# A mixer's queries, keys and decays in three tiles instead of one, another order of its score levels, and waits by tile for reused pool space

## The chip, the cores and the metric

The kernel runs on one core of a Trainium2 chip, in one launch. The metric is the device time of an execution in microseconds (us). Before the change it is 1374.46 us, the median of three runs (1373.4 to 1375.46). One more execution was profiled; its own time is 1371.81 us, of which the profile's span covers 1370.0 us.

In the profile PE is TensorE's matmul side and PEld its weight loads, DVE is VectorE, ACT is ScalarE, POOL is GpSimd, and SP is the engine whose queue issues most DMAs. L729 is line 729 of the kernel.

## The reference, cut to what matters

One layer of a streaming encoder runs on a prompt of 1024 tokens and, with its own stored states, on 32 further tokens (the decode rows). All in float32:

```python
h, st_new = mixer(rms_norm(x, g_mix_pre[l]), st, ...)      # in-projection, three kinds of heads, out-projection
x = x + rms_norm(h, g_mix_post[l])
h, ffn_buf = conv_ffn(rms_norm(x, g_ffn_pre[l]), ...)      # up, causal conv of 3, gelu(gate) * value, down
x = x + rms_norm(h, g_ffn_post[l])
```

Six GLA heads and five HGRN2 heads share one recurrence with a decay per key channel, computed in blocks of 64 tokens:

```python
b = jnp.cumsum(ac, axis=1)
diff = b[:, :, None] - b[:, None, :]
decay = jnp.where(mask, jnp.exp(jnp.where(mask, diff, 0.0)), 0.0)
scores = jnp.einsum('bihd,bjhd,bijhd->bijh', qc, kc, decay)
o = (jnp.einsum('bijh,bjhv->bihv', scores, vc)
     + jnp.einsum('bihk,bhkv->bihv', qc * jnp.exp(b), s))
s_new = (jnp.exp(b_last)[..., None] * s
         + jnp.einsum('bjhk,bjhv->bhkv', kc * jnp.exp(b_last[:, None] - b), vc))
```

Five mLSTM heads have a scalar decay per token, a normaliser and a running maximum. Each kind's output is normalised per head and gated; the three together (`cat`) go through `w_out`.

## The kernel before, in words

Every large product is made of three fp32r products, high by high, low by high and high by low (lines 101 to 103), so PE carries about 11,500 matmuls.

**Stages.** The tokens are cut into units of 128: u = 0 to 7 of the prompt, and u = 8, the 32 decode rows. Units 0 to 2, 3 to 5, and 6, 7 and 8 are three groups. `inproj` (from line 357) normalises and projects a group and writes its queries, keys and decays to DRAM (`qkb_d`, or `qkbs_d` for unit 8). `mixer(u)` (from line 719) is a generator; its pieces are merged into the program beside the in-projection of the next group, and those of the last group (in the order u8, u6, u7) beside the out-projection (`outproj`, from line 1055). Then come the FFN's up-projection and down-projection. Matmuls of a mixer are queued with `soon` and taken one by one between those of the large products. The order on each engine is fixed when the program is built, by a scheduler that works with a model of the durations; every engine then takes its own instructions strictly in that order, and waits in front of the first that isn't ready.

**A mixer.** Lines 727 to 731 load one tile `qkb` (1536 columns, one buffer) by two DMAs, first the decays `b`, then queries `q` and keys `k` together; slices of it are called q4, k4 and b4. ACT takes eb = exp(b) (L771), DVE forms kh (L787, L790) and qz = q*eb (L781), and ACT makes `qe`, four scaled copies of parts of q (L812, one buffer). The scores are built by levels: level c pairs the second half of each block of 2c tokens with its first half. `operands(c)` (lines 814 to 840) subtracts decays on DVE (L825), takes two exponentials on ACT (L827, L828), and writes Ld (L830) and Qz (L835, L839); level 1 needs one exponential (L833, L834), and PE reads its keys straight from k4. The levels are taken in pairs, since there are two buffers of Qz and Ld. PE multiplies (L717) and DVE puts a level's result into P by `copy_predicated` (L805). After the last pair come z = q*k for the diagonal (L930), og and oh (the outputs, from P and from the states), om and oi (the mLSTM heads), and `finish` (squares L988, sums L989, POOL's reciprocal root L220 and L221, gated `cat` L991 and L993). Two heads' results are kept in the same PSUM banks, so om waits until og has been read by DVE (L991).

**Names that the prediction uses.** pv and pf are PSUM banks of the in-projection, pb transposes values vf (ACT copies them at L468) that had been projected in the other orientation; vth, vg and g_d are the gates on their way to DRAM (L427, L429, L431, L432), which a mixer loads again as gt (L743). wt_* are in-projection weights, wor the out-projection's (L689, eight loads of 512 KB), split into woh (ACT, L107 and L1049) and wol (DVE, L110 and L1051). ctp, ch and cl are the transposed `cat` (L1075, L1079, L1080), zp the out-projection's banks, z0, z1 their contents, fxt the transposes of the result. jk is the discarded output of the Square that gives a unit's norm (L303); gh is a broadcast row of gains.

Of the kernel before, what the change touches and what calls it, by code (L numbers as in the profile page):

```python
# [8 lines left out]
F32 = mybir.dt.float32  # L9
F32R = mybir.dt.float32r  # L10
BF16 = mybir.dt.bfloat16
# [3 lines left out]
PSUM = bass.MemoryType.PSUM  # L15
# [18 lines left out]
SUBS = [(0, 272), (272, 256)]  # L34
# [5 lines left out]
def fcol(u):  # L40
# [51 lines left out]
def body(ctx: ExitStack, tc: tile.TileContext, a: dict):  # L92
    nc = tc.nc
    act, dve, pool, pe, sp = nc.scalar, nc.vector, nc.gpsimd, nc.tensor, nc.sync
# [19 lines left out]


    dr = ctx.enter_context(tc.tile_pool(name="dr", bufs=1, space=DRAM))
    cp = ctx.enter_context(tc.tile_pool(name="cp", bufs=1))
    psb = ctx.enter_context(tc.tile_pool(name="psb", bufs=3, space=PSUM))
    mxs = ExitStack()
    mx = mxs.enter_context(tc.tile_pool(name="mx", bufs=1, side="left"))  # L120
    psm = mxs.enter_context(tc.tile_pool(name="psm", bufs=2, space=PSUM))
    pfs = ExitStack()
    pf = pfs.enter_context(tc.tile_pool(name="pf", bufs=1, side="left"))
    p1s = ExitStack()
    p1 = p1s.enter_context(tc.tile_pool(name="p1", bufs=1, side="right"))
# [131 lines left out]
    pws, wo_raw, ring = ExitStack(), [], []  # L257
# [99 lines left out]
    def inproj(g, xh, xl, normed, scaled=None):  # L357
# [4 lines left out]
        def t1(tag, bufs=1, w=T, dt=F32):  # L362
            return pf.tile([128, w], dt, tag=tag, name=f"{tag}_{g}", bufs=bufs)
# [290 lines left out]
        q = t1("q", 2)  # L654
# [4 lines left out]
        for t, f in ((4, 1), (5, 2)):  # L659
            ps = feat(t)  # L660
            q = t1("q", 2)
# [5 lines left out]
        q = t1("q", 2)  # L667
# [12 lines left out]

        if g == 2:
            pfs.close()
            pw = pws.enter_context(tc.tile_pool(name="pw", bufs=1, side="left"))
            ring.append(lambda name: pw.tile([128, 1024], F32, tag="ring", name=name, bufs=NRING))
            for k in range(8):
                if k == CT0:
                    load_cat(0)
                wo_raw.append(ring[0](f"wor{k}"))
                sp.dma_start(wo_raw[k], a["w_out"][k])  # L689
# [29 lines left out]
    def mixer(u, g, ci0):  # L719
        n = 128 if u < 8 else DEC  # L720
# [3 lines left out]
        nch = len(chunks)  # L724
        levels = [c for c in LEVELS if 2 * c <= cl]

        qkb = mx.tile([128, 1536], F32, tag="qkb", name=f"qkb{u}", bufs=1)
        for s0, s1 in ((2, 3), (0, 2)):
            sp.dma_start(qkb[:, 4 * n * s0:4 * n * s1],  # L729
                         (qkb_d[u] if u < 8 else qkbs_d)[:, s0:s1].rearrange("p a f n -> p (a f n)"))  # L730
# [11 lines left out]
        gt = mx.tile([128, 1024], F32, tag="gt", name=f"gt{u}", bufs=1)  # L742
# [65 lines left out]
        qe = mx.tile([128, 2, 2, 128], F32, tag="qe", name=f"qe{u}", bufs=1)  # L808
# [46 lines left out]
        cat = mx.tile([128, 1024], F32, tag="cat", name=f"cat{u}", bufs=1) if u != 7 else ring[0]("cat7")  # L855
# [563 lines left out]
    praw, ph, EARLY = [], [], 3  # L1419
# [79 lines left out]
    def down_all(ph, pc, begun, late):  # L1499
# [6 lines left out]
        ssp = late.enter_context(tc.tile_pool(name="p11", bufs=1, side="right"))  # L1506

        def w_banks(name):
            return [psf.tile([128, 512], F32, tag="sx", name=f"{name}0", bufs=1)] + \
# [74 lines left out]
        s1 = psf.tile([128, 512], F32, tag="xw", name="s1", bufs=4)  # L1584
# [55 lines left out]

        run("P7", X, False, True, lambda p, w: residual(p))
        late.close()
        px_ = late.enter_context(tc.tile_pool(name="p12", bufs=1, side="right"))
        xres = {}
        for u in range(4):
            xres[u] = px_.tile([128, 1024], F32, name=f"fr{u}")
# [31 lines left out]
    side = []  # L1678
# [34 lines left out]
        side.append(mixers(g))  # L1713
    p1s.close()
    p2s = ExitStack()
    p2 = p2s.enter_context(tc.tile_pool(name="p2", bufs=1, side="right"))
    wo = outproj_setup(p2)
    wo += (out_weights(wo),)
    p3s = ExitStack()

    x0 = p3s.enter_context(tc.tile_pool(name="p3", bufs=1, side="right")).tile([128, 8, 2, SUBS[0][1]], F32, name="xg0")
    xlate[0] = x0
    n0, n1 = SUBS[0][1], SUBS[1][1]
    smp = DEC // 2
# [11 lines left out]


    p4s, p5s, p6s, p7s, p8s, p9s, pxs, phs, late = (ExitStack() for _ in range(9))
    p0 = p4s.enter_context(tc.tile_pool(name="p4r", bufs=1, side="left"))
    p4 = p4s.enter_context(tc.tile_pool(name="p4", bufs=1, side="left"))  # L1740
    px = [pxs.enter_context(tc.tile_pool(name=f"px0{i}", bufs=1, side="left")) for i in range(2)]
    psf = p4s.enter_context(tc.tile_pool(name="psf", bufs=1, space=PSUM))
    praw += [p0, p4]
    upper.append(psf)
    raw0 = up_raw(0)
    pt = p5s.enter_context(tc.tile_pool(name="p5", bufs=1, side="left"))
    tail.append(lambda name: pt.tile([128, 1024], F32, tag="tail", name=name, bufs=3))
    own = {"c1": pt.tile([128, SUBS[0][1]], F32, name="c1_00")}
    jks.append(own["c1"].bitcast(BF16)[:, :512])
# [14 lines left out]
        with tc.issue_after(kept["c1"].ins):  # L1764
            next(last[1])
    p3s.close()
    tp = p6s.enter_context(tc.tile_pool(name="p6", bufs=1, side="left"))
# [5 lines left out]
    p7 = p7s.enter_context(tc.tile_pool(name="p7", bufs=1, side="right"))  # L1773
# [7 lines left out]
    for u in uus[0]:  # L1781
        pool.memset(u[:, 0:2], 0.0)
    p7.tile([128, 8], F32, name="pad1")
    px1 = p8s.enter_context(tc.tile_pool(name="px1", bufs=1, side="right"))
    py = []
    X.append(None)
    begun = {}

    def freed():
        pxs.close()  # L1790
        ph.append(phs.enter_context(tc.tile_pool(name="ph", bufs=1, side="left")))
# [10 lines left out]
    for i, _ in enumerate(up_all(pw_, W0, X, uus, lambda: py[0], freed, ahead, blk)):  # L1802
        if i == 1:

            with tc.issue_after(done[0].ins), tc.issue_after(kept["c6"].ins):
                for x in last:
                    next(x)
            X[1] = col_operands([px1] * 2, {f"B{k + 1}{j + 1}": x1[:, 4 * k:4 * k + 4, j, :] for k in range(2) for j in range(2)}, 1)
            p6s.close()
            p5s.close()  # L1810
            py.append(p9s.enter_context(tc.tile_pool(name="p9", bufs=1, side="right")))
    sp.dma_start(a["p_fc"], fhalo)
    sp.dma_start(a["q_fc"], fcache)
    p9s.close()
    p8s.close()
    p7s.close()
    p10 = p8s.enter_context(tc.tile_pool(name="p10", bufs=1, side="right"))
    down_all(ph[0], p10, begun, late)
    late.close()
    p8s.close()  # L1820
# [131 lines left out]
```

## Time and profile before

| what | before |
|---|---|
| time, median of 3 runs | 1374.46 us (1373.4 to 1375.46) |
| time of the profiled execution | 1371.81 us |
| its span | 1370.0 us |
| PE busy | 1309.2 us, 96% of the span |
| PEld, DVE, ACT, POOL busy | 1191.7, 1030.3, 704.6 and 329.9 us |
| in-projection with the mixers of units 0 to 5 | to about 513 us |
| out-projection with the mixers of units 8, 6 and 7 | about 513 to 655 us |
| FFN | from about 682 us to the end |

A row of the timeline gives start and length in us, engine, line, operation and tiles, and in square brackets how long the engine had been idle before it and what it waited for. PEclk is the clock granted to TensorE as a share of full speed.

### The profile page before, as it was taken

Reading aid. Unit: us, or ns where it says so; the run is one execution under the profiler, and the core shown is the slowest. Engines: PE = TensorE matmul, PEld = TensorE weight load, DVE = VectorE, ACT = ScalarE, POOL = GpSimd, SP = SyncE. Lnnn points to the kernel's source line nnn. Section 1 sums busy time; section 2 is a strip of 40 time slices with the busy share of each in tenths; the row PEclk is TensorE's granted clock in tenths of the full one; section 3 lists DMA queues with packets and bytes.
Section 4 is the critical chain, followed back from the end, with each engine's and each line's share of the span. In section 5 each row is a group of like instructions: output and inputs, shape, how many; then the busy total and the mean of one; then the engine's idle time right before and its main releaser. Section 6 shows DMA issues by size and latency. Waiting matters only on the chain.

```text
span 1370.0 us, 29214 instructions
## 1 busy us (share of the span) xinstructions
PE 1309.2 (96%) x11472; PEld 1191.7 (87%) x11472; DVE 1030.3 (75%) x1916; ACT 704.6 (51%) x1368; POOL 329.9 (24%) x529
## 2 busy tenths in 40 slices
PE   6999999998998989998989999999999999999997
PEld 5999989998897977777889999999999997678885
DVE  4786559678597757796788888888888876399566
ACT  4555556555474535353665455545555544454552
POOL 5532403135022154133231112121121110010005
PEclk9999999999999999999999999999999999999999
DMA  9599878786789935535413465555365239644425
GB/s 344 204 322 352 288 270 252 266 281 219 261 247 315 328 102 202 158 115 155 149 43 132 145 176 149 150 137 161 111 171 136 85 131 390 262 156 134 149 105 123
DMA packets 125825, 269.72 MB, mean 197 GB/s; under 512 B 24007, under 2 KB 59367, under 8 KB 125607
## 3 DMA queue, kind: packets, MB, share of 16 engines
q1 hardware_dynamic: 111959, 245.43, 52.4%
q0 software_dynamic: 8928, 18.09, 7.2%
q10 hardware_dynamic: 4800, 4.33, 0.9%
q8 instruction: 90, 1.47, 0.4%
q14 instruction: 48, 0.39, 0.1%
HBM read 206.72 MB, written 86.18 MB: 214 GB/s over the span
## 4 chain that ended last, share of the span: by engine, by line
PE 65%; DVE 13%; DMA 8%; ACT 7%; issue 3%; POOL 3%; SPq 1%; ACTq 0%; DVEq 0%; POOLq 0%
PE pux L103 5%; PE pux L102 5%; PE pux L101 5%; PE puw L102 3%; PE puw L103 3%; PE puw L101 3%; PE q L101 3%; PE q L102 3%; PE q L103 3%; PE pv L101 3%; PE pv L103 2%; PE x L101 2%; DMA qkb<-qkb_d 2%; PE pv L102 2%; PE x L102 2%
## 5 line engine op out<-in xcount | busy, mean ns | idle before, releaser
L1375 DVE SCALAR_TENSOR_TENSOR y<-uu,fconv_sb,y 128x1060 f32<-128x1060 f32 x88 | 116.3, 1321 | 37.0 <-ACT y L1373 36.5
L1311 ACT COPY c<-pux 128x272 f32<-128x272 f32 (+1 forms) x132 | 49.3, 375 | 49.7 <-PE pux L103 49.0
L101 PE MATMUL pv<-wt_0h,xh 128*128 128x256 f32 (+2 forms) x195 | 57.5, 295 | 6.0 <-ACT xh L321 2.6
L101 PE MATMUL zp<-woh,ch 128*128 128x512 f32 (+1 forms) x144 | 59.1, 411 | 2.6 <-issue 1.4
L1373 ACT ACTIVATE y<-uu,fconv_sb 128x1060 f32<-128x1060 f32 x44 | 56.0, 1273 | 7.8 <-POOL uu L1369 7.5
L103 PE MATMUL zp<-woh,cl 128*128 128x512 f32 (+1 forms) x144 | 57.7, 401 | 1.3 <-DVE cl L1080 1.3
L1372 POOL COPY fhalo<-uu 128x2 f32<-128x2 f32 x44 | 16.5, 375 | 174.5 <-DVE uu L1316 174.4
L102 PE MATMUL zp<-wol,ch 128*128 128x512 f32 (+1 forms) x144 | 58.0, 402 | 0.0
L103 PE MATMUL pv<-wt_0h,xl 128*128 128x256 f32 (+2 forms) x195 | 56.0, 287 | 0.2 <-DVE xl L322 0.2
L103 PE MATMUL pv<-wt_1h,xl 128*128 128x256 f32 (+2 forms) x195 | 56.1, 288 | 0.0
L102 PE MATMUL pv<-wt_0l,xh 128*128 128x256 f32 (+2 forms) x195 | 55.9, 287 | 0.1
L101 PE MATMUL pv<-wt_1h,xh 128*128 128x256 f32 (+2 forms) x195 | 55.7, 286 | 0.0
L102 PE MATMUL pv<-wt_1l,xh 128*128 128x256 f32 (+2 forms) x195 | 55.6, 285 | 0.0
L1551 POOL TENSOR_TENSOR gss<-gss 128x1 f32<-128x1 f32 (+1 forms) x9 | 8.3, 923 | 186.4 <-ACT gjk L1544 186.4
L220 POOL TENSOR_SCALAR hrs<-hss 128x5 f32<-128x5 f32 (+3 forms) x27 | 10.7, 396 | 175.9 <-DVE hss L989 175.2
L805 DVE COPY_PREDICATED P<-masks_sb,sc 128x352 f32<-128x352 int32 (+3 forms) x53 | 37.8, 714 | 11.8 <-PE sc L717 10.7
L101 PEld LDWEIGHTS pv<-wt_0h,xh 128*128 128x128 f32 (+1 forms) x195 | 36.8, 189 | 8.1 <-ACT xh L321 3.3
L431 POOL TENSOR_TENSOR vg<-vth,gh 128x256 f32<-128x256 f32 (+1 forms) x36 | 28.6, 796 | 59.4 <-DVE vth L427 34.3
L1369 POOL COPY uu<-uu 128x2 f32<-128x2 f32 x44 | 31.4, 714 | 43.6 <-DVE uu L1316 42.7
L221 POOL TENSOR_TENSOR hrs<-hrs,mhalf 128x5 f32<-128x5 f32 (+3 forms) x27 | 39.3, 1454 | 2.3
L993 POOL TENSOR_TENSOR cat<-cat,gt 128x320 f32<-128x320 f32 (+3 forms) x27 | 31.3, 1161 | 29.5 <-DVE cat L991 29.4
L102 PEld LDWEIGHTS pv<-wt_0l,xh 128*128 128x128 f32 (+1 forms) x195 | 36.9, 189 | 0.6 <-POOL wt_0l L110 0.5
(1714 smaller groups left out, 5330.7 us busy)
## 6 DMA issues: line engine op xcount, KB each, us to landing
wrP<-in_w_dn SPq DMA_DIRECT2D x27, 512.0 KB, 3.3
h_d<-y SPq DMA_DIRECT2D x22, 530.0 KB, 2.8
ht<-h_d SPq DMA_DIRECT2D x22, 530.0 KB, 7.8
wt_0r<-in_w_tok SPq DMA_DIRECT2D x21, 512.0 KB, 11.2
wt_1r<-in_w_tok SPq DMA_DIRECT2D x21, 512.0 KB, 5.1
ws_d<-in_w_dn POOLq DMA_DIRECT2D x20, 512.0 KB, 9.6
wrP<-ws_d SPq DMA_DIRECT2D x20, 512.0 KB, 4.5
wt_0l<-lt_d SPq DMA_DIRECT2D x14, 512.0 KB, 7.6
```

The lines of the kernel that those rows point to most:

```text
L101: pe.matmul(ps, lh[0], rh[0], start=first, stop=False, **kw)
L102: pe.matmul(ps, lh[0], rh[1], start=False, stop=False, **kw)
L103: return pe.matmul(ps, lh[1], rh[0], start=False, stop=last, **kw)
L221: pool.tensor_tensor(out, out, mhalf[:n, :cols], op=ALU.pow)
L431: pool.tensor_tensor(o[:n], th[:n], gh[:n, c0:c0 + 256], op=ALU.mult)
L805: dve.copy_predicated(dst, mk.broadcast_to([n, 11, *mk.shape[2:]]), src)
L993: pool.tensor_tensor(cat[:n, c0:c0 + 64 * nh], cat[:n, c0:c0 + 64 * nh], gt[:n, c0:c0 + 64 * nh], op=ALU.mult)
L1311: kept[name] = act.copy(t, ps)
L1369: pool.tensor_copy(u[:, GAP_P:GAP_P + 2], u[:, GAP_S - 2:GAP_S])
L1372: behind["POOL"] = pool.tensor_copy(fhalo[:, j, :], u[:, NCOL - 2:NCOL])
L1373: act.activation(y, u, AF.Identity, scale=fconv[:, j, 2:3], bias=fconv[:, j, 3:4])
L1375: dve.scalar_tensor_tensor(y, uu[i][:, s:s + NCOL], fconv[:, j, s:s + 1], y, op0=ALU.mult, op1=ALU.add)
```

## The change

It has four parts.

- **Tiles.** q, k and b become three tiles of 512 columns with a DMA each, in the order q, b, k. q has two buffers, k and b have one. The sizes of the pool allow it because gh moves from the pool `mx` to `p1`, and the Squares' jk of units 3 to 8 moves from a buffer of its own in `p1` into the one buffer of `qe` (unit 2's uses k's).
- **Levels.** 32, 16 | 8, 4 | 2, 1 becomes 32, 16 | 2, 1 | 8, 4. For unit 8, whose blocks are 32 long, 16, 8 | 4, 2 | 1 becomes 16, 2 | 1, 8 | 4.
- **Waits.** Every pool gets `reuse_waits="tile"`: a tile on space of a closed pool waits for the tiles that lay there.
- **Order.** The scheduler gives another order with these: 771 of 9677 PE rows move, 470 of 1918 on DVE, 190 of 1352 on ACT, 21 of 534 on POOL, and SP has nine more DMAs and 60 rows moved. All lies before the FFN's up-projection, whose order and that of everything behind it is as before. The instructions of compute are otherwise the same in kind and number. Lines from 731 on have one number less.

```diff
-LEVELS = [32, 16, 8, 4, 2, 1]
+LEVELS = [32, 16, 2, 1, 8, 4]
...
-    mx = mxs.enter_context(tc.tile_pool(name="mx", bufs=1, side="left"))
+    mx = mxs.enter_context(tc.tile_pool(name="mx", bufs=1, side="left", reuse_waits="tile"))
...
-    gh = mx.tile([128, 1024], F32, name="gh")
+    gh = p1.tile([128, 1024], F32, name="gh")
...
-                jk = mx.tile([128, 1024], BF16, tag=("gt", "cat", "qkb")[u], name=f"jk{u}", bufs=1)
+                jk = mx.tile([128, 1024], BF16, tag=("gt", "cat", "k")[u], name=f"jk{u}", bufs=1)
             else:
-                jk = p1.tile([128, 1024], BF16, tag="jk", name=f"jk{u}", bufs=1)
+                jk = mx.tile([128, 1024], BF16, tag="qe", name=f"jk{u}", bufs=1)
...
-        qkb = mx.tile([128, 1536], F32, tag="qkb", name=f"qkb{u}", bufs=1)
-        for s0, s1 in ((2, 3), (0, 2)):
-            sp.dma_start(qkb[:, 4 * n * s0:4 * n * s1],
-                         (qkb_d[u] if u < 8 else qkbs_d)[:, s0:s1].rearrange("p a f n -> p (a f n)"))
-        q4, k4, b4 = (qkb[:, 4 * n * i:4 * n * (i + 1)].rearrange("p (f n) -> p f n", n=n) for i in range(3))
+        q4, k4, b4 = (mx.tile([128, 512], F32, tag=t, name=f"{t}{u}", bufs=1 + (t == "q"))[:, :4 * n]
+                      .rearrange("p (f n) -> p f n", n=n) for t in ("q", "k", "b"))
+        for i, t in ((0, q4), (2, b4), (1, k4)):
+            sp.dma_start(t, (qkb_d[u] if u < 8 else qkbs_d)[:, i])
```

The other pools, the FFN's among them, get the same argument as `mx`.

The order changes at three places. In the names below a number behind a letter is the unit (qe5), and the last number counts tiles.

**ACT, about 425 to 442 us of the profile before.** Units 3 to 5 have been projected, unit 5's mixer begins. wt2_* are weights of the third group, og4 and oh4 the outputs of unit 4. Before:

```order
L468 COPY vf1_5766<-pv2_1_0_5767 128x288
L337 CAST wt2_3_0h_6035<-wt2_3_0r_6033 128x1024
L812 ACTIVATE qe5_6129<-qkb5_6017,cf_sb_111 128x128 x4
L988 ACTIVATE sq4_0_5883<-og4_5793 128x384
L988 ACTIVATE sq4_6_5890<-oh4_5794 128x320
L771 ACTIVATE eb5_6089<-qkb5_6017 128x512
L337 CAST wt2_3_1h_6041<-wt2_3_1r_6039 128x1024
L789 ACTIVATE kh5_6099<-kh5_6099 128x512
L468 COPY vf1_5766<-pv2_1_1_5857 128x288
```

After:

```order
L525 ACTIVATE fr_2_4634<-fr_2_4634 64x288
L811 ACTIVATE qe5_6147<-q5_6032,cf_sb_111 128x128 x4
L337 CAST wt2_2_0h_5914<-wt2_2_0r_5912 128x1024
...
L468 COPY vf1_5781<-pv2_1_0_5782 128x288
L337 CAST wt2_3_0h_6053<-wt2_3_0r_6051 128x1024
L987 ACTIVATE sq4_0_5898<-og4_5808 128x384
L987 ACTIVATE sq4_6_5905<-oh4_5809 128x320
L770 ACTIVATE eb5_6107<-b5_6034 128x512
L788 ACTIVATE kh5_6117<-kh5_6117 128x512
L337 CAST wt2_3_1h_6059<-wt2_3_1r_6057 128x1024
L468 COPY vf1_5781<-pv2_1_1_5872 128x288
```

The copies qe5 have gone about a dozen rows up, out of the row of instructions ahead of the second vf1 copy; eb5 still stands ahead of it, and kh5 before the cast. On SP the load of q5 now stands about 65 rows ahead of that of b5, and b5 sixteen rows earlier than the first load of qkb5 did.

**PE, the end of unit 7's mixer, about 625 to 642 us.** Before (mi are state products, w7 the mLSTM weights):

```order
L717 MATMUL oh7_8206<-S7_0_8185,qz_153 64x64
L717 MATMUL mi_158<-vm0_157,kw2_156 64x65 x10
L1181 MATMUL fxt81_8465<-ident_122,z8_8082 128x32 x4
L717 MATMUL om7_8311<-vm0_157,w7_7915 64x65 x10
L101 MATMUL zp50_8486<-woh_6857,ch50_8419 128x512
```

After:

```order
L717 MATMUL oh7_8233<-S7_0_8212,qz_153 64x64
L717 MATMUL mi_158<-vm0_157,kw2_156 64x65 x10
L103 MATMUL zp40_8412<-woh_6875,cl41_8366 128x512
L1074 MATMUL ctp50_8441<-ident_122,ct5_8221 128x128 x4
L101 MATMUL zp41_8450<-woh_6875,ch40_8228 128x512
...
L103 MATMUL zp41_8450<-woh_6875,cl41_8366 128x512
L717 MATMUL om7_8338<-vm0_157,w7_7942 64x65 x10
```

One zp40 matmul, a transposition and the 24 matmuls of zp41 now stand between oh7's last matmul and om7. Likewise 23 matmuls of zp40 now stand between unit 7's last scores and og7, where one transposition (fxt80) stood. Units 8 and 6 finish earlier in the row of zp banks too.

**SP, the loads at the start of the out-projection, about 512 to 529 us.** Before:

```order
L689 DMA wor6_5750<-in_w_out 128x1024
L980 DMA out_q_gh<-S8_0_7135 128x256
L689 DMA wor7_5752<-in_w_out 128x1024
L270 DMA ct1_6865<-cat_d_83 128x1024
L729 DMA qkb6_7305<-qkb_d_75 128x512
L729 DMA qkb6_7305<-qkb_d_75 128x1024
L277 DMA xr0_6904<-in_xp 128x1024
L739 DMA v6_7313<-v_d_81 128x704
L743 DMA gt8_6896<-g_d_82 32x1024
```

After:

```order
L979 DMA out_q_gh<-S8_0_7156 128x256
L689 DMA wor6_5765<-in_w_out 128x1024
L738 DMA v6_7337<-v_d_81 128x704
L1038 DMA gm_6877<-in_grows 128x1024
L730 DMA q7_7874<-qkb_d_75 128x512
L742 DMA gt8_6917<-g_d_82 32x1024
L689 DMA wor7_5767<-in_w_out 128x1024
```

The last piece of the out-projection's weights, wor7, now stands behind v6, q7 and gt8. On ACT and DVE the last of the gates, vth8_7, which gt8 waits for, now stands ahead of the casts of woh and of all of wol; before it stood behind seven casts of woh and seven rows of wol. ACT also has sq8, eb6, kh6 and unit 6's first exponentials between the casts of woh and the first copy of zp00, where it had qe6 alone.

More of the change, by code (lines that the diff above doesn't have):

```diff
@@ L682, in inproj @@
             pfs.close()
-            pw = pws.enter_context(tc.tile_pool(name="pw", bufs=1, side="left"))
+            pw = pws.enter_context(tc.tile_pool(name="pw", bufs=1, side="left", reuse_waits="tile"))
             ring.append(lambda name: pw.tile([128, 1024], F32, tag="ring", name=name, bufs=NRING))
@@ L1505, in down_all @@
         act.activation(gp[:, 512:], gp[:, 512:], AF.Copy, scale=-1.0)
-        ssp = late.enter_context(tc.tile_pool(name="p11", bufs=1, side="right"))
+        ssp = late.enter_context(tc.tile_pool(name="p11", bufs=1, side="right", reuse_waits="tile"))
         def w_banks(name):
@@ L1642, in down_all @@
         late.close()
-        px_ = late.enter_context(tc.tile_pool(name="p12", bufs=1, side="right"))
+        px_ = late.enter_context(tc.tile_pool(name="p12", bufs=1, side="right", reuse_waits="tile"))
         xres = {}
@@ L1715, in body @@
     p2s = ExitStack()
-    p2 = p2s.enter_context(tc.tile_pool(name="p2", bufs=1, side="right"))
+    p2 = p2s.enter_context(tc.tile_pool(name="p2", bufs=1, side="right", reuse_waits="tile"))
     wo = outproj_setup(p2)
@@ L1719, in body @@
     p3s = ExitStack()
-    x0 = p3s.enter_context(tc.tile_pool(name="p3", bufs=1, side="right")).tile([128, 8, 2, SUBS[0][1]], F32, name="xg0")
+    x0 = p3s.enter_context(tc.tile_pool(name="p3", bufs=1, side="right", reuse_waits="tile")).tile([128, 8, 2, SUBS[0][1]], F32, name="xg0")
     xlate[0] = x0
@@ L1738, in body @@
     p4s, p5s, p6s, p7s, p8s, p9s, pxs, phs, late = (ExitStack() for _ in range(9))
[L1739 to L1742, printed above, removed]
+    p0 = p4s.enter_context(tc.tile_pool(name="p4r", bufs=1, side="left", reuse_waits="tile"))
+    p4 = p4s.enter_context(tc.tile_pool(name="p4", bufs=1, side="left", reuse_waits="tile"))
+    px = [pxs.enter_context(tc.tile_pool(name=f"px0{i}", bufs=1, side="left", reuse_waits="tile")) for i in range(2)]
+    psf = p4s.enter_context(tc.tile_pool(name="psf", bufs=1, space=PSUM, reuse_waits="tile"))
     praw += [p0, p4]
@@ L1745, in body @@
     raw0 = up_raw(0)
-    pt = p5s.enter_context(tc.tile_pool(name="p5", bufs=1, side="left"))
+    pt = p5s.enter_context(tc.tile_pool(name="p5", bufs=1, side="left", reuse_waits="tile"))
     tail.append(lambda name: pt.tile([128, 1024], F32, tag="tail", name=name, bufs=3))
@@ L1766, in body @@
     p3s.close()
-    tp = p6s.enter_context(tc.tile_pool(name="p6", bufs=1, side="left"))
+    tp = p6s.enter_context(tc.tile_pool(name="p6", bufs=1, side="left", reuse_waits="tile"))
     x1 = tp.tile([128, 8, 2, n1], F32, name="xg1")
@@ L1772, in body @@
     p2s.close()
-    p7 = p7s.enter_context(tc.tile_pool(name="p7", bufs=1, side="right"))
+    p7 = p7s.enter_context(tc.tile_pool(name="p7", bufs=1, side="right", reuse_waits="tile"))
     pw_.append(p7)
@@ L1783, in body @@
     p7.tile([128, 8], F32, name="pad1")
-    px1 = p8s.enter_context(tc.tile_pool(name="px1", bufs=1, side="right"))
+    px1 = p8s.enter_context(tc.tile_pool(name="px1", bufs=1, side="right", reuse_waits="tile"))
     py = []
@@ L1790, in freed @@
         pxs.close()
-        ph.append(phs.enter_context(tc.tile_pool(name="ph", bufs=1, side="left")))
+        ph.append(phs.enter_context(tc.tile_pool(name="ph", bufs=1, side="left", reuse_waits="tile")))
         ph[0].tile([128, 8], F32, name="pad")
@@ L1810, in body @@
             p5s.close()
-            py.append(p9s.enter_context(tc.tile_pool(name="p9", bufs=1, side="right")))
+            py.append(p9s.enter_context(tc.tile_pool(name="p9", bufs=1, side="right", reuse_waits="tile")))
     sp.dma_start(a["p_fc"], fhalo)
@@ L1816, in body @@
     p7s.close()
-    p10 = p8s.enter_context(tc.tile_pool(name="p10", bufs=1, side="right"))
+    p10 = p8s.enter_context(tc.tile_pool(name="p10", bufs=1, side="right", reuse_waits="tile"))
     down_all(ph[0], p10, begun, late)
```

10 lines of the change are left out of this document (5 added, 5 removed).

## The prediction

> **What bounds the kernel now.** First the page: the busy times.
>
> ```profile
> PE 1309.2 (96%) x11472; PEld 1191.7 (87%) x11472; DVE 1030.3 (75%) x1916; ACT 704.6 (51%) x1368; POOL 329.9 (24%) x529
> ```
>
> PE is the bound, and the change leaves it the same matmuls. The busy time includes time at a lower clock. So the change can win only PE's idle time, 1370.0 - 1309.2 = 61 us less the modelled ends, and what the clock costs behind it. The second view is the table of windows (first the length, then busy time of PE, PEld, DVE, ACT and POOL, granted clock, DMA share, GB/s):
>
> ```profile
> 100.00:300.00 200.00, 195.80 (x2097) 186.75 (x2096) 136.42 (x293) 111.00 (x217) 48.74 (x71) 0.99 0.85 288
> 300.00:400.00 100.00, 95.49 (x1280) 86.82 (x1279) 75.06 (x188) 56.46 (x125) 32.39 (x43) 1.00 0.73 241
> 400.00:450.00 50.00, 42.37 (x603) 38.95 (x601) 41.30 (x102) 26.23 (x62) 12.56 (x21) 0.93 0.91 306
> 450.00:500.00 50.00, 45.68 (x667) 42.04 (x666) 32.15 (x90) 24.56 (x65) 15.73 (x21) 0.98 0.65 226
> 500.00:550.00 50.00, 46.78 (x352) 37.72 (x352) 37.53 (x83) 26.61 (x57) 24.61 (x29) 0.95 0.51 172
> 600.00:650.00 50.00, 44.65 (x571) 36.42 (x566) 38.63 (x86) 20.13 (x47) 14.90 (x25) 0.98 0.41 122
> 700.00:1100.00 400.00, 400.00 (x3302) 400.00 (x3301) 334.27 (x552) 208.10 (x355) 72.55 (x181) 1.00 0.49 137
> ```
>
> From 700 to 1100 PE has no idle time, and the order there is unchanged: nothing is to be had. In the quoted windows from 300 to 650 PE idles 4.5, 7.6, 4.3, 3.2 and 5.4 us, 25 us together. That is the stretch whose order moves. Third, the waits from 300 to 700 (total, times, longest), with one row that counts:
>
> ```profile
> ACT qe L812 <- DMA qkb<-qkb_d: 26.5, 4, 8.6
> ```
>
> ACT waits 26.5 us for the load, in four units. The timeline ties the longest of these to PE, ACT first, then PE:
>
> ```profile
> 427.29 1.05 ACT L337 CAST wt_0h<-wt_0r 128x1024 fp32r<-128x1024 f32 x1 [0.53 <-PE pv L102]
> 436.56 1.28 ACT L812 ACTIVATE qe<-qkb,cf_sb 128x128 f32<-128x128 f32 x4 [8.22 <-DMA qkb<-qkb_d]
> 439.22 0.62 ACT L771 ACTIVATE eb<-qkb 128x512 f32<-128x512 f32 x1
> 441.21 0.39 ACT L468 COPY vf<-pv 128x288 f32<-128x288 f32 x1
> ```
>
> ```profile
> 436.32 0.29 PE L102 MATMUL pv<-xl,wt_1h 128*128 128x288 f32 x1
> 436.45 0.29 PE L103 MATMUL pv<-xh,wt_1l 128*128 128x288 f32 x1
> ...
> 441.65 1.33 PE L455 MATMUL pb<-ident,vf 128*128 128x128 f32 x5 [4.39 <-ACT vf L468]
> ...
> 443.02 0.44 PE L102 MATMUL pv<-xl,wt_0h 128*128 128x288 f32 x1
> 443.26 0.44 PE L103 MATMUL pv<-xh,wt_0l 128*128 128x288 f32 x1
> ```
>
> qe5 stands at the head of ACT's row for 8.22 us; the vf copy that PE needs (L468, 441.21) stands behind it.
>
> **The change part by part**, against the profiled execution's 1371.81 us; the median of the runs is 2.65 us above that, and I carry the difference over to it.
>
> *Unit 5's load.* Before it goes out here (SP's queue), behind the last reader of unit 4's tile and behind everything else on SP:
>
> ```profile
> 412.34 2.11 SPq L331 DMA_DIRECT2D wt_0r<-in_w_tok  x1
> 429.41 0.42 SPq L729 DMA_DIRECT2D qkb<-qkb_d  x1
> DMA to landing us min/median/max: 5.5/5.6/5.9
> ```
>
> (The third row is of the tile's own view.) q5 now goes out a mixer ahead, and b5 stands ahead of the row at 412.34, so both land by about 412 + 5.6 = 418, before ACT, which is through with its cast at 428.3, comes to them. The 8.22 us vanish. PE's idle 4.39 goes, and the clock with it: two matmuls are 0.24 us apart at 443.02 against 0.13 at 436.32, and this lasts from 441.65 to about 446.9, 5.2 us x (1 - 0.13/0.24) = 2.4 us. Together 6.8 us. What is late next: sq4_0 and sq4_6 must wait for unit 4's outputs, and eb5 (0.62), kh5 (about as long) and a cast (1.05) still stand ahead of vf. I leave 0.8 us of wait: **-6.0** (bounds -6.8 and, if sq4 is as late as the load was, 0).
>
> *Unit 7's end.* Two waits and a third:
>
> ```profile
> 623.54 0.92 PE L717 MATMUL og<-v,P 64*64 64x64 f32 x24 [0.91 <-DVE P L805]
> 629.35 0.80 PE L717 MATMUL om<-vm,w 64*64 64x65 f32 x20 [1.82 <-DVE cat L991]
> ...
> 641.14 0.39 PE L103 MATMUL zp<-woh,cl 128*128 128x512 f32 x1
> 641.36 0.39 PE L101 MATMUL zp<-woh,ch 128*128 128x512 f32 x1
> ...
> 647.30 0.50 PE L103 MATMUL zp<-woh,cl 128*128 128x512 f32 x1 [1.26 <-DVE cl L1080]
> ```
>
> zp matmuls start 0.22 to 0.23 us apart. The 23 now ahead of og7 are 5.1 us and the 24 ahead of om7 5.3 us, over waits of 0.91 and 1.82: **-2.7**. The wait at 647.30 stays, as ctp60, ctp61 and zp60 still follow each other; so does its half clock (the window 646 to 656 below). Bounds -2.7 and 0.
>
> *Unit 3.* ACT's qe waits there as well, 5.82 us until 316.38, and PE then waits 3.4 us in three pieces:
>
> ```profile
> 316.38 1.28 ACT L812 ACTIVATE qe<-qkb,cf_sb 128x128 f32<-128x128 f32 x4 [5.82 <-DMA qkb<-qkb_d]
> 331.69 0.81 PE L717 MATMUL oi<-C,mqz 128*64 128x65 f32 x20 [0.97 <-DVE cat L991]
> 334.68 0.66 PE L318 MATMUL xt<-ident,x 128*128 128x128 f32 x4 [0.74 <-ACT vth L113]
> 338.80 0.40 PE L101 MATMUL pv<-wt_0h,xh 128*128 128x282 f32 x1 [1.73 <-ACT vth L113]
> ```
>
> Fifteen us lie between, so only part comes from the load. Between 0 and -3.4 I take half: **-1.7**.
>
> *The wait at 498 (unit 8).* PE has 2.91 us and a half clock behind it, and DVE stands for a load shortly before:
>
> ```profile
> 498.37 0.58 PE L101 MATMUL pv<-xh,wt_0h 128*128 128x288 f32 x1 [2.91 <-DVE vth L427]
> ```
>
> ```profile
> 494.34 0.36 DVE L920 TENSOR_TENSOR C<-C,dcs 128x195 f32<-128x195 f32 x1 [4.43 <-DMA C<-in_s_c]
> ```
>
> This is unit 8's state C. Its load now stands ahead of one of the two ab6 loads, and on DVE the product with C stands one row ahead of the last operation on hn5, which the gating of unit 5 needs. What the earlier load gives, that row takes: **0** (bounds -4.6, the wait and 1.7 of clock, and +1).
>
> *Levels.* They are the same six; the pair scored last has one exponential more and the middle pair one less. This moves a few tenths, and the bounds are wider than that: **0**, bounds ±1.
>
> *Nine more DMAs.* They take 0.42 us of SP each (the row at 429.41), 3.8 us over nine mixers. Only a load that PE waits for could feel it; such loads are priced below: **0**.
>
> *Start of the out-projection.* wor7 now goes out behind gt8, which waits for the last gate to be in DRAM:
>
> ```profile
> 513.27 0.66 PE L1075 MATMUL ctp<-ident,ct 128*128 128x128 f32 x4 [0.83 <-ACT vth L113]
> 515.31 0.77 PE L101 MATMUL zp<-woh,ch 128*128 128x512 f32 x1 [1.38 <-issue]
> ```
>
> ```profile
> 513.96 0.37 SPq L689 DMA_DIRECT2D wor<-in_w_out  x1
> ...
> 528.49 0.32 SPq L743 DMA_DIRECT2D gt<-g_d  x1
> ```
>
> ```profile
> L1051 DVE TENSOR_TENSOR wol<-wor,woh x6: 1207/1218/1225, 517.9 to 523.8; 128x1024 fp32r<-128x1024 f32 x6
> DMA to landing us min/median/max: 6.6/6.6/6.6
> ```
>
> (These two are of wor's own view.) Before, gt8 went out at 528.49 and the gate stood behind seven rows of wol, 7 x 1.22 = 8.5 us. Without these gt8 goes out near 520, or 518 as the casts of woh are out of its way too, and wor7 behind it, where it went at 514. With 6.6 to land, 1.05 for woh and 1.22 for wol its halves are there at 527 to 529. PE comes to them after some 42 of the 48 matmuls of zp00 and zp01, 9.5 us after 514.5. A new wait of about 3 us with 1.7 of clock, against 0.83 + 1.38 us and some 1.5 of clock (the zp at 515.31 is 0.77 long) that are there now and go: 4.7 - 3.7 = **+1**; bounds -3.7, and +12.7 with gt8 as late as before: 528.49 + 8.9 is 13 us behind 524, 3.4 of clock follow, and 3.7 go.
>
> The clock is weighed here, since it doubles the price of a short wait:
>
> ```profile
> 498.00:502.00 4.00, 3.63 (x17) 3.66 (x18) 3.94 (x12) 1.29 (x6) 3.32 (x5) 0.57 0.54 197
> 646.00:656.00 10.00, 8.74 (x35) 6.99 (x34) 8.70 (x13) 3.66 (x7) 0.74 (x2) 0.83 0.80 249
> ```
>
> 0.17 x 10 = 1.7 us are lost from 646 to 656, where PE's longest wait is 1.26 us. The Trainium skill ("TensorE: Matmul & The Clock Gate", Part 1) has the clock fall to half after at least one idle window of about 3.4 us. This row speaks against that as a condition: waits far below it were enough. By the page the new wait would cost 3 us alone, and the sum would be 1.7 lower.
>
> *Other waits the change adds.* k and b have one buffer, so b of the next unit waits on SP for the last pair's subtraction, with weights queued behind it. The Squares of units 3 to 5 come ahead of qe0 on ACT, so unit 0's levels start some 30 us later, where DVE has room (136 of 200 us busy from 100 to 300, in the windows). The waits by tile can only shorten waits at closed pools. Bounds 0 and +6; near the small end, since PE idles 4.2 of 200 us there: **+1**.
>
> Sum: -6.0 - 2.7 - 1.7 + 1 + 1 = **-8.4 us**: 1363.4 for a profiled execution, **1366** by the median.
>
> **The rivals.**
>
> *More is won.* Also the waits at 498, 513 and 331 go with their clock: -6.8 - 2.7 - 3.4 - 4.6 - 3.7 = -21 us, 1353. For it: the order of the change covers units 8 and 6 better too. Against: loads and gates still decide there. Chance 0.12.
>
> *The wait only moves.* PE reaches unit 8 some 7 us sooner, but the loads of S and C and the gates, which end the waits at 482 and 498, don't come sooner, as their links run over DVE (DVE is busy 32 of 50 us there) and SP. Then 5.5 of the 8.4 are given back: 1371.5. Chance 0.2.
>
> *Slower.* gt8 holds SP until 528, because the gate's store or v6 is as late as before, and wor7's halves are there at 537: PE waits 13 us in front of the last pieces of zp00 and zp01, 3.4 us of clock follow, and the 9.4 of the other terms and the 3.7 of the old waits don't pay for it: +3.3, 1377.8. Each us of gt8 costs one, so it decides from about 525 on. For it: SP takes its rows in turn, and ACT has sq8, eb6 and kh6 behind woh7's cast, ahead of the copies that empty zp00. Against: the gate was moved ahead of the casts. Chance 0.18.
>
> **How the numbers follow.** The forecast has 0.5 and covers 1360 to 1370. Less than 0.2% (2.7 us) can't be told from no change here. Faster: 0.5 + 0.12 + half of the third case = 0.72 (0.1); the other half is "same", 0.1, and slower is 0.18. The range of 1353 to 1379 takes in the two middle cases, most of the larger gain and the slower case as far as its price goes.
>
> **What would show it.** The row of qe5 without a wait and pb's wait under 1 us; no half clock from 440 to 447; og7 and om7 without waits; qe3 without a wait. For the slower case: the issue of the last wor behind 525, and zp waiting for woh or wol around 525 to 535. I am wrong if the window 400 to 450 keeps 7 us of PE's idle time, or if a window up to 300 gains more than 2 us of it.

## The result, and the profile after

The changed kernel takes 1364.85 us (median of 6 runs, 1360.13 to 1365.64) against 1374.49 us (6 runs, 1373.4 to 1375.59): a ratio of 0.9922, 95% interval 0.9908 to 0.9936, 9.6 us less. The forecast was 1366 us, 8.4 us less. The profiled execution took 1360.13 us, the quickest of the six, with a span of 1358.4 us.

The page and the windows of the changed kernel:

```profile
PE 1307.1 (96%) x11472; PEld 1191.5 (88%) x11472; DVE 1027.1 (76%) x1916; ACT 707.3 (52%) x1368; POOL 323.8 (24%) x529
```

```profile
100.00:300.00 200.00, 199.09 (x2192) 189.71 (x2191) 137.81 (x299) 112.91 (x221) 50.59 (x73) 1.00 0.86 294
300.00:400.00 100.00, 95.79 (x1282) 87.97 (x1283) 77.67 (x196) 59.79 (x132) 31.76 (x44) 1.00 0.73 242
400.00:450.00 50.00, 43.80 (x591) 40.40 (x590) 41.20 (x106) 27.53 (x64) 11.04 (x20) 0.93 0.93 332
450.00:500.00 50.00, 48.31 (x665) 44.56 (x663) 30.62 (x89) 22.88 (x61) 20.93 (x28) 0.97 0.58 196
500.00:550.00 50.00, 46.63 (x366) 36.71 (x366) 43.09 (x93) 29.08 (x61) 20.75 (x27) 0.93 0.57 182
600.00:650.00 50.00, 46.52 (x388) 38.14 (x388) 33.86 (x58) 18.90 (x36) 12.40 (x21) 1.00 0.54 156
```

Nearly the same busy time on every engine, less idle time on PE. But the window that was to gain most, 400 to 450, still lacks 6.2 us of PE and has the same clock, and the one from 100 to 300, to which I gave a loss of 1 us, is now full but for 0.9 us. Fixed windows shift against the program, though. A sharper view is the start of the same matmul in both traces (the n-th of its line and bank's name):

| up to | start before, us | after minus before | in this stretch | forecast for it |
|---|---|---|---|---|
| a pv matmul of the second group | 300.0 | -3.6 | -3.6 | +1 |
| a pf matmul of the third | 400.1 | -4.7 | -1.1 | -1.7 |
| the first zp matmul | 515.3 | -7.1 | -2.4 | -6.0 |
| a late zp matmul | 657.0 | -10.0 | -2.9 | -1.7 |
| the down-projection's first | 1160.1 | -10.0 | 0.0 | 0 |
| a later one of it | 1300.1 | -11.6 | -1.6 | 0 |

The total was met with two misses in it that offset each other, so that it came out so near is partly luck. The traces also show more than the medians: the changed kernel's profiled execution is 4.7 us below the median of its runs, that of before 2.65 us below.

One statement about the change doesn't hold in the traces: the order at the FFN's start is not as before. In the profile before, two matmuls of pux stand between the first of puw and the others (692.54 and 695.18 us), in the changed kernel twelve (684.04 and 687.21). From about 719 us of before (709 after) the order on the engines of compute is the same. The stretch that holds this came out even.

The first hoped-for effect is there. ACT's waits at qe in the changed kernel, total, times and longest (33.6 us for the load in the whole profile before):

```profile
ACT qe L811 <- DVE Qz L838: 4.8, 6, 1.6
```

Unit 5's start, ACT first, then PE:

```profile
411.49 1.28 ACT L811 ACTIVATE qe<-q,cf_sb 128x128 f32<-128x128 f32 x4
...
431.36 0.62 ACT L770 ACTIVATE eb<-b 128x512 f32<-128x512 f32 x1
...
433.34 0.40 ACT L468 COPY vf<-pv 128x288 f32<-128x288 f32 x1
```

```profile
434.72 0.82 PE L455 MATMUL pb<-ident,vf 128*128 128x128 f32 x6
442.64 0.40 PE L103 MATMUL pv<-xh,wt_0l 128*128 128x288 f32 x1 [1.88 <-DMA wt_0l<-lt_d]
...
446.77 0.40 PE L103 MATMUL pv<-xh,wt_1l 128*128 128x288 f32 x1 [1.15 <-DMA wt_1l<-lt_d]
```

qe5 runs 25 us earlier without a wait, vf is copied in time and pb doesn't wait. The half clock behind pb's wait is gone too (1.00 in the window 440 to 450 below). Two other things take most of this back. The first lies ahead of it: PE waits 2.11 us for DVE at 417, and the half clock that keeps the window 400 to 450 at 0.93 stands behind this wait:

```profile
417.27 1.14 PE L717 MATMUL sc<-Qz,Ld 64*64 64x64 f32 x64 [2.11 <-DVE e L530]
```

```profile
416.00:426.00 10.00, 8.73 (x131) 8.12 (x132) 8.97 (x19) 2.80 (x7) 0.39 (x2) 0.66 0.86 286
440.00:450.00 10.00, 6.96 (x93) 6.03 (x88) 6.92 (x24) 6.81 (x16) 0.06 (x1) 1.00 1.03 409
```

That is 0.34 x 10 = 3.4 us of clock. Before, PE had waits of 1.02 and 1.14 us between 420 and 430, at full clock. The second thing is the weights' low halves, which are now late. They were issued behind the out-projection's first six weight loads (SP's queue):

```profile
427.64 3.96 SPq L689 DMA_DIRECT2D wor<-in_w_out  x6
...
432.43 0.40 SPq L335 DMA_DIRECT2D wt_0l<-lt_d  x1
```

10 us from the issue at 432.43 to the matmul at 442.64, with 3 MB ahead of it. Unit 7's end has no wait in front of og and om:

```profile
608.19 0.91 PE L717 MATMUL og<-v,P 64*64 64x64 f32 x24
...
618.08 0.80 PE L717 MATMUL om<-vm,w 64*64 64x65 f32 x20
```

And wor7 comes in time. gt8 goes out at 512.60; on ACT the cast waits for it, on PE nothing does (PE's wait there is for qz of unit 8):

```profile
512.60 0.32 SPq L742 DMA_DIRECT2D gt<-g_d  x1
513.01 0.38 SPq L689 DMA_DIRECT2D wor<-in_w_out  x1
```

```profile
516.88 1.05 ACT L1048 CAST woh<-wor 128x1024 fp32r<-128x1024 f32 x1 [2.63 <-DMA wor<-in_w_out]
```

```profile
508.24 1.22 PE L101 MATMUL zp<-woh,ch 128*128 128x512 f32 x2 [1.98 <-DVE qz L780]
```

### The profile page after: what moved, and what is told of

It is laid out like the page before. It is cut to its first block, busy times and chain, and to the rows that moved or that the text cites. A ratio compares the mean times of both kernels' runs of the same rounds, so it can differ in the third digit from the quotient of the medians.

```text
span 1358.4 us, 29238 instructions
## 1 busy us (share of the span) xinstructions
PE 1307.1 (96%) x11472; PEld 1191.5 (88%) x11472; DVE 1027.1 (76%) x1916; ACT 707.3 (52%) x1368; POOL 323.8 (24%) x529
## 4 chain that ended last, share of the span: by engine, by line
PE 60%; DVE 8%; DMA 4%; ACT 2%; issue 2%; POOL 1%; SPq 0%; DVEq 0%; POOLq 0%; ACTq 0%
PE pux L101 5%; PE pux L102 5%; PE pux L103 5%; PE puw L102 3%; PE puw L101 3%; PE puw L103 3%; PE q L101 3%; PE q L102 3%; PE q L103 3%; PE x L101 2%; PE x L102 2%; PE x L103 2%; PE puy L102 2%; PE puy L103 2%; PE puz L101 2%
## 5 line engine op out<-in xcount | busy, mean ns | idle before, releaser
L220 POOL TENSOR_SCALAR hrs<-hss 128x5 f32<-128x5 f32 (+3 forms) x27 | 11.6, 430 | 177.7 <-DVE hss L988 175.4
L103 PEld LDWEIGHTS pv<-wt_0h,xl 128*128 128x128 f32 (+1 forms) x195 | 37.0, 190 | 0.6 <-DVE xl L322 0.4
L103 PEld LDWEIGHTS pv<-wt_1h,xl 128*128 128x128 f32 (+1 forms) x195 | 36.5, 187 | 0.8 <-DVE xl L322 0.3
```

The source lines that it names most:

```text
L103: return pe.matmul(ps, lh[1], rh[0], start=False, stop=last, **kw)
```

## Experiments

Twelve kernels, each timed in five rounds against the kernel before. In these sets the kernel before spread from 1368 to 1381 us, so one ratio holds to about 0.15%, some 2 us; what a place gained is read from the traces, by the start of the same matmul as above. An edit can also change the scheduler's order. By the traces e3, f4 and h2 have the order of before on every engine and e4 that of the changed kernel; e2 and h1 have one of their own, alike in both, and so has each of e1 and f1.

### The parts alone

**e1_tiles**, the tiles without the other two:

```diff
-        qkb = mx.tile([128, 1536], F32, tag="qkb", name=f"qkb{u}", bufs=1)
+        q4, k4, b4 = (mx.tile([128, 512], F32, tag=t, name=f"{t}{u}", bufs=1 + (t == "q"))[:, :4 * n] ...
```

> The three tiles alone (q in two buffers, jk in qe's buffer, gh moved), with the levels in the order of before and the waits of before. Theory A (the gain comes from loads that no longer hold the head of ACT's row, and from where mixers' pieces then stand in PE's row): most of the 9.6 us, 1365 to 1369 us. Theory B (the order of the levels makes it): 1373 to 1376. Theory C (the waits by tile make it): 1373 to 1376.

**e2_levels**:

```diff
-LEVELS = [32, 16, 8, 4, 2, 1]
+LEVELS = [32, 16, 2, 1, 8, 4]
```

> The order of the levels alone (32, 16, 2, 1, 8, 4), with one tile qkb. Theory A: within 2 us of before, 1372.5 to 1376.5. Theory B: 1365 to 1369. Theory C: as before.

**e3_waits**: `reuse_waits="tile"` in every pool of the kernel before.

> The waits by tile alone; the order on every engine is that of before, only waits at reused pool space go. Theory A: 0 to -1 us, 1373.5 to 1374.5. Theory B: the same. Theory C: 1365 to 1369.

**e4_tiles_levels**: the changed kernel without `reuse_waits="tile"`.

> Tiles and levels, without the waits by tile: the order is that of the changed kernel. Theory A: as the changed kernel within 1 us, 1364 to 1366. Theory B: the same. Theory C: 1372 to 1375.

Measured: tiles 0.9984 (0.9969 to 0.9999), levels 0.9973 (0.9957 to 0.9988), waits 0.9984 (0.9971 to 0.9998), tiles and levels 0.9950 (0.9935 to 0.9964). As times: 1372.7, 1370.2, 1372.8 and 1369.1. **None of the three theories holds.** The tiles, on which I had put nearly everything, give 2 us alone; the levels give most of the three, though the intervals overlap; and the waits by tile, worth nothing in my sum, separate 1369.1 from 1364.85, in the same order and with intervals that just touch. By place, minus the first profile of before:

| kernel | at 300 | at 400 | first zp (515) | 657 | span |
|---|---|---|---|---|---|
| e1 tiles | -3.7 | -2.8 | +5.9 | +5.4 | +4.1 |
| e2 levels | -3.3 | -2.4 | -3.8 | -3.0 | -1.8 |
| e3 waits | 0.0 | +2.1 | +1.8 | +0.1 | -1.8 |
| e4 tiles, levels | -3.4 | -2.9 | +0.1 | -1.5 | -2.2 |
| changed | -3.6 | -4.7 | -7.1 | -10.0 | -11.7 |
| before, second profile (f4) | +1.8 | +1.4 | +1.1 | +2.6 | +4.5 |

The last row is the caution: two profiles of one kernel differ by 4.5 us. The profile of e1 is of an execution 3.2 us above its median. Two places stand out beyond that. The gain up to 300 comes with the tiles and with the levels, each alone. And between 400 and 515 the tiles alone lose 8.7 us, tiles and levels lose 3.0, and only the waits by tile added to them give a gain; the levels alone gain 1.4. PE's wait there, in e1 and in e4:

```profile
452.87 0.61 PE L103 MATMUL pv<-xh,wt_0l 128*128 128x288 f32 x1 [9.09 <-DMA wt_0l<-lt_d]
```

```profile
447.37 0.61 PE L103 MATMUL pv<-xh,wt_0l 128*128 128x288 f32 x1 [4.82 <-DMA wt_0l<-lt_d]
```

It is the wait of 1.88 us of the changed kernel. SP's queue in e4, and what its rows of wor waited for:

```profile
433.69 2.81 SPq L689 DMA_DIRECT2D wor<-in_w_out  x6
...
437.09 0.39 SPq L335 DMA_DIRECT2D wt_0l<-lt_d  x1
```

```profile
SPq L689 <- DMA mqk_d<-y: 2.1, 1, 2.1
SPq L689 <- DMA mqks_d<-y: 1.5, 1, 1.5
```

The tiles wor lie where the pool of the in-projection's feature stage (`pf`) lay. Without the argument the first of them waits until the last stores of that pool's tiles to DRAM have landed, 3.6 us, and SP stands: wt_0l goes out at 437.09 and not at 432.43, 4.7 us later, and PE starts its matmul 4.7 us later (447.37 and 442.64). Not all of this is the wait's. SP's row ahead of wor goes out 2.4 us later in e4 as well, and PE is 1.8 us behind at 430, after a half clock at 336 that only the profile of e4 has. PE's own wait is 2.9 us longer. With the argument the changed kernel shows no such row; the first load follows its predecessor at once (427.64).

### The order of the levels

Why would an order of six equal levels move the first 300 us? In the profile before ACT waits for unit 1's load too, with a copy behind it that the in-projection needs, and PE waits later:

```profile
195.13 1.28 ACT L812 ACTIVATE qe<-qkb,cf_sb 128x128 f32<-128x128 f32 x4 [5.79 <-DMA qkb<-qkb_d]
196.42 0.47 ACT L637 COPY fr<-pf 64x384 f32<-64x384 f32 x1
```

```profile
230.56 0.45 PE L101 MATMUL pf<-xh,wf_11h 128*128 128x384 f32 x1 [1.89 <-DVE q L545]
```

The load waits for the last reader of unit 0's tile. In the old order this is PE, which in the last pair reads level 1's keys straight from it; DVE was through with the tile at 177.6:

```profile
187.19 0.67 PE L717 MATMUL sc<-Qz,qkb 64*64 64x64 f32 x32
```

```profile
188.27 0.87 SPq L729 DMA_DIRECT2D qkb<-qkb_d  x2
```

Two kernels were to tell that from a mere reshuffle:

```diff
-LEVELS = [32, 16, 8, 4, 2, 1]
+LEVELS = [32, 16, 8, 1, 4, 2]
```

> The kernel before with the levels 32, 16, 8, 1, 4, 2: level 1, the one whose keys PE reads straight from the tile qkb, moves to the middle pair, and the last pair is 4, 2. Theory K (PE's reading of k4 in the last pair is what releases the tile late, and with it the next unit's load, at whose wait ACT stands): as levels alone, 1369 to 1372; qe of unit 1 waits under 1 us, and PE's wait at 231 us under 1 us. Theory O (the other order of the levels only moves instructions about, which pair holds level 1 doesn't matter): 1372 to 1376, or alike in this kernel and the next.

```diff
-LEVELS = [32, 16, 8, 4, 2, 1]
+LEVELS = [32, 16, 4, 2, 8, 1]
```

> The kernel before with the levels 32, 16, 4, 2, 8, 1: another order, but level 1 stays in the last pair. Theory K: nothing is won, 1373 to 1376; qe of unit 1 waits about 6 us and PE 1.9 us at 231. Theory O: alike with the kernel that has level 1 in the middle.

Measured: 0.9990 (0.9976 to 1.0004), 1372.95 us, and 0.9993 (0.9977 to 1.0008), 1374.48 us. The times don't tell the two apart. Theory K's time for the first was missed, and qe of unit 1 waits 1.02 us there, a little over its limit; theory O's times hold for both. The second kernel is also no reshuffle: it has the order of before, and the first that of e2. What speaks for theory K is the release itself. With level 1 in the middle DVE is the last reader, and the load goes out 10.5 us earlier:

```profile
176.90 0.28 DVE L835 TENSOR_TENSOR Qz<-x,qkb 128x128 f32<-128x128 f32 x1
```

```profile
177.78 0.86 SPq L729 DMA_DIRECT2D qkb<-qkb_d  x2
```

ACT's waits at qe, and PE's at the matmul above, level 1 in the middle:

```profile
ACT qe L812 <- DMA qkb<-qkb_d: 15.3, 5, 4.9
```

```profile
228.91 0.44 PE L101 MATMUL pf<-xh,wf_11h 128*128 128x384 f32 x1 [0.72 <-DVE q L545]
```

and with level 1 in the last pair:

```profile
ACT qe L812 <- DMA qkb<-qkb_d: 32.3, 6, 8.5
```

```profile
232.79 0.69 PE L101 MATMUL pf<-xh,wf_11h 128*128 128x384 f32 x1 [1.90 <-DVE q L545]
```

At 300 the first is 3.0 us ahead of the profile before and the second 3.4 behind; the 3.4 are half clocks (0.83 at 155 to 165 and at 225 to 245, where the profile before has 0.91 in the later window). So the release is shown: the place of the level that reads k4 on PE sets when the tile comes free. That PE's shorter wait at 229 follows from ACT's shorter one at qe is argued, since 35 us lie between and the order changed too. Later the first kernel gives part back: it meets the same wait for wt_0l as e4 (5.25 us at 446), and from 657 to 760 it loses 3.9 us at the FFN's start (more on that below).

### q in one buffer

```diff
-bufs=1 + (t == "q"))
+bufs=1)
```

> The changed kernel with one buffer for q instead of two, so that q is loaded when the mixer before is through with it. Theory A (the early load of q frees the head of ACT's row, and that is a large part of the gain): qe5 waits over 4 us again and 4 to 7 us are lost, 1369 to 1372. Theory S (the gain of units 3 to 5 comes from what SP issues and when, not from q): 1364 to 1367.

Measured: 0.9983 (0.9966 to 1.0000), 1372.8 us; 8 us of the 9.6 are gone, a little over what theory A said. Its sign isn't there: qe5 waits 2.54 us and not over 4, and the longest wait below is unit 7's. PE's wait near 446 is for weights:

```profile
ACT qe L811 <- DMA q<-qkb_d: 9.3, 4, 5.9
```

```profile
446.78 0.40 PE L103 MATMUL pv<-xh,wt_0l 128*128 128x288 f32 x1 [3.57 <-DMA wt_0l<-lt_d]
```

At 300 it is 1.1 us ahead and not 3.6 (PE waits 0.74 us at 229, as in the changed kernel, but with a half clock, and 1.07 us at 156), at the first zp 0.8 and not 7.1. With one buffer most of the gain is gone; how much of that is the buffer and how much the other order that this kernel has isn't shown. That pb waits for vf again isn't so either. The profile is of an execution 3.3 us above its median.

From 657 to 760 this kernel loses 5.4 us more at the FFN's start. Its order there is another than in the kernel before and in the changed one. PE is idle 2.8 us longer than in the profile before, with waits of 2.50 us at 680 and of 3.12 at 692, and loses 3.4 us more to half clocks (0.74 from 680 to 700, against 0.83 before):

```profile
691.74 0.58 PE L101 MATMUL puy<-B21h,A_0h 128*128 128x256 f32 x1 [3.12 <-ACT B21h L1227]
```

The losses there go with the order: 5.4 us in f1, 3.9 in h1, 2.7 in e2 and 0.6 in e1, which each have another; all others have the order of before or of the changed kernel there and lie between a gain of 0.7 and a loss of 1.7, the latter in the second profile of before.

### The out-projection's weights

Here SP issues wor0 to wor5 later. In the first kernel they go behind the fifth block's weights (`wl_last` is the load of its last low half):

```diff
-                wo_raw.append(ring[0](f"wor{k}"))
-                sp.dma_start(wo_raw[k], a["w_out"][k])
...
+                if blk == WOB:
+                    for k in range(8):
+                        if k == CT0:
+                            load_cat(0)
+                        wo_raw.append(ring[0](f"wor{k}"))
+                        with tc.issue_after(wl_last[0].ins):
+                            sp.dma_start(wo_raw[k], a["w_out"][k])
```

> The changed kernel with the six loads of 512 KB of the out-projection's weights (wor0 to wor5) fourteen rows further down SP's queue, behind the in-projection weights of that stretch. Theory S (the waits by tile earn by what stands behind these loads; the 1.88 and 1.15 us that PE still waits for in-projection weights, and the half clock there, come from the 3 MB ahead of them): 3 to 6 us less than the changed kernel, 1359 to 1362. Theory P (the waits by tile earn elsewhere, and these waits are for something else): as the changed kernel, 1364 to 1366.

The second is the same without the waits by tile:

> Tiles and levels without the waits by tile, and with wor0 to wor5 fourteen rows further down SP's queue. Theory S: the wait of the first of these loads for reused pool space then holds nothing that PE needs, and most of what the waits by tile give is here without them: 1360 to 1364. Theory P: as tiles and levels alone, 1368 to 1370.

In the third, WOB is 6 and not 5:

> The changed kernel with wor0 to wor5 further down SP's queue still, behind the weights of the sixth block (some 470 us), where the DMA engines were 34 to 44% busy from 470 to 500. Theory S (these 3 MB cost PE where they meet weights and gates on full DMA engines): no wait over 2 us between 440 and 470, and 3 to 5 us less than the changed kernel, 1360 to 1362. Theory R (what is won there is lost again by what comes late next): 1364 to 1368.

and in the fourth they are spread:

```diff
+    WOS = {4: (0,), 5: (1, 2), 6: (3, 4), 7: (5, 6, 7)}
...
+                for k in WOS.get(blk, ()):
```

> The changed kernel with these loads spread, one or two behind each block's weights. Theory S: 1360 to 1363. Theory R: 1364 to 1368.

Measured: 0.9946 (0.9929 to 0.9964), 1367.6 us; 0.9952 (0.9934 to 0.9969), 1368.2; 0.9946 (0.9929 to 0.9963), 1367.5; and spread 0.9911 (0.9894 to 0.9928), 1363.4. The first is at neither theory's time, the second at theory P's, the third at theory R's, the last between. Theory S is half right. The waits for wt_0l go in all of them; but moved as a block the loads delay what comes next, and 2.7 and 2.6 us are lost against the changed kernel (first and third; the intervals overlap a little). The half clock that the first text puts at these waits stands earlier, behind the wait at 417, and f2 has one there as well (0.83 from 416 to 426). f2, then g1, DVE and PE, then the spread kernel:

```profile
461.76 0.69 PE L721 MATMUL mi<-ident,mqk 128*128 128x128 f32 x2 [5.47 <-ACT kt L869]
```

```profile
482.64 0.42 DVE L905 TENSOR_TENSOR S<-S,dec 128x256 f32<-128x256 f32 x1 [10.32 <-DMA S<-in_s_gh]
```

```profile
484.47 0.81 PE L721 MATMUL oi<-C,mqz 128*64 128x65 f32 x10 [8.47 <-DVE cat L994]
```

```profile
477.82 0.80 PE L721 MATMUL om<-vm,w 64*64 64x65 f32 x20 [2.66 <-DVE cat L994]
```

The load of S is that of unit 8, issued behind the block. In f2 it is the load of gt for which ACT stood:

```profile
460.96 0.74 ACT L869 COPY kt<-mi 64x256 f32<-64x256 f32 x2 [5.92 <-DMA gt<-g_d]
```

Spread out, a wait of 2.66 us is left. That kernel's interval overlaps the changed kernel's, so it isn't shown to be better, but it is the best of all.

With the loads late, leaving the waits by tile away costs 0.6 us (f7 against f2, less than the intervals tell) and not 4.2 (e4 against the changed kernel, 0.9950 and 0.9922). Both pairs have the same order. That fits their gain coming from this one row of SP's queue. But f7 is hardly better than e4 (1368.2 and 1369.1): what the late loads win at wt_0l is lost behind them, where PE waits 5.89 us at 464.

### The same kernel again

No edit.

> The kernel before, unchanged, as a kernel of its own: what two sets of runs of one kernel differ by, and a second profile of it. All theories: ratio 0.999 to 1.001, and the waits of the profile at 231, 338, 441, 498 and 515 us again.

Measured: 0.9998 (0.9978 to 1.0017), 1374.55 us. Its waits at 231, 340, 442, 499 and 516 are there again, of 1.89, 1.73, 3.51, 3.36 and 1.39 us.

## Why the prediction was right, and where it wasn't

- **Unit 5's load, -6.0.** The mechanism was right, as qe5 and vf show; the size wasn't. From 400 to the first zp 2.4 us are gained. The step that failed is "I leave 0.8 us of wait": I asked what else ACT had ahead of vf, not what PE needed besides. That was wt_0l and wt_1l, behind wor on SP, whose two waits take 3.0 us; and an operand from DVE at 417, whose wait of 2.11 us brings 3.4 us of clock. That wait goes with the levels: e2 has it too (2.13 us at 419.5).
- **The wait at 498, 0.** It is gone, and so is one of 1.41 us at 482. In their place came 1.53 us at 486, with a half clock (0.83 from 484 to 494).
- **Waits by tile, no term.** "The waits by tile can only shorten waits at closed pools" is true, and it left out a price. SP's rows of wor waited 3.2 us in the profile before as well, hidden under PE's wait for vf. With that gone they would have set the time: without the waits by tile (e4) this stretch loses 3.0 us.
- **Levels, 0.** Wrong. I counted instructions and not who reads the tile last. With level 1 out of the last pair the tile comes free earlier; this, or the second buffer of q, goes with the 3 us won up to 300. I had the row of waits for 300 to 700, where 26.5 of the 33.6 us lie, and didn't look at the rest. The sign by which the text said it would be wrong, more than 2 us up to 300, is there.
- **Other waits, +1.** None showed. Up to 300 the loads and Squares cost PE nothing.
- **Unit 7's end, -2.7, and the out-projection's start, +1.** Together -2.9 measured against -1.7. og7 and om7 don't wait, as worked out. But PE has waits of 1.06 us at 527 and 1.17 at 635 that the sum lacks, and the old waits at 513 and 515 that the second term counts lie in the stretch before; so that the sums are near says little. At the start gt8 went out at 512.6 and not at 518 to 520 (its estimate took only the rows of wol away; the start had moved 7 us too), so wor7 cost PE nothing. The wait of 1.98 us there is for another thing, with a half clock about it (the window 500 to 550 has 0.93).
- **Unit 3, -1.7.** 1.1 measured, 0.7 against the second profile of before; but the mechanism failed. qe3 doesn't wait, and PE's three waits are there all the same, 0.90, 0.72 and 1.40 us where they were 0.97, 0.74 and 1.73. So the load wasn't what held them, and the near size is luck. The last of them in the changed kernel:

```profile
334.78 0.40 PE L101 MATMUL pv<-wt_0h,xh 128*128 128x282 f32 x1 [1.40 <-DVE xl L322]
```

- **The last 1.6 us** of the profile's 11.7 aren't the change's; they are a half clock that one execution had and the other not (below).
- **Clock.** The price that the rows gave, 1.7 us behind a short wait, held at 486; at 417 and 508 it was 3.4 us (0.66 from 505 to 515), and behind the 1.88 us at 442 nothing. By the rule of the Trainium skill ("TensorE: Matmul & The Clock Gate", Part 1) waits under 3.4 us wouldn't bring it; in the changed kernel waits of 1.53 and 1.98 us, at 486 and 508, have it.

What the runs leave open: how the loss at the FFN's start in f1, h1 and e2 divides between their order there and the half clock; how ACT's wait at qe reaches PE at 231; and how much the second buffer of q gives without another order.

## What to carry to other kernels

When a wait at the head of an engine's row is taken away, look at the bound engine's next two operands and at what stands ahead of *their* loads: here a pool's reuse held the queue and had been hidden. Of a tile loaded once per step, look up its last reader on every engine; to move that one reader forward can be worth as much as a second buffer (some 3 us up to 300 here, either way). Moving a block of large loads moves the wait to whatever stands behind it; spreading them did best here, though not by more than the intervals tell. And when a scheduler makes the order, compare it over the whole program: an edit in the mixers changed it at the FFN's start.

## What the runs showed of the hardware

A short wait brings a half clock in some executions and not in others. Two places with the same waits, in the profile before and after (PEclk is the sixth number after the window's length, 1.00 or 0.72):

```profile
72.00:78.00 6.00, 5.55 (x34) 5.28 (x34) 5.93 (x6) 1.44 (x2) 4.73 (x2) 1.00 1.03 382
1172.00:1178.00 6.00, 4.77 (x14) 3.48 (x13) 1.90 (x3) 1.66 (x3) 0.00 (x0) 0.72 1.03 414
```

```profile
72.00:78.00 6.00, 5.40 (x22) 5.41 (x23) 5.93 (x6) 1.44 (x2) 4.80 (x2) 0.72 1.01 370
1162.00:1168.00 6.00, 4.77 (x24) 2.71 (x23) 2.36 (x4) 2.77 (x5) 0.00 (x0) 1.00 1.01 403
```

PE waits 1.91 us at 72.5 and 1.23 us at 1174 (1164 after) in both. Each time it costs 0.28 x 6 = 1.7 us. The change isn't the reason: the second profile of the kernel before, with the same order and a wait of 1.90 us there, has the half clock at the first place:

```profile
72.00:78.00 6.00, 5.03 (x20) 5.03 (x21) 5.57 (x6) 1.77 (x3) 4.98 (x2) 0.72 1.00 366
```

Comparing two single profiles, such a place can't be told from a gain; this second profile is 4.5 us longer than the first.
